# A two-block transformer on one core: `ada` sums of gMLP in later columns, residual tiles split where they are made, and VectorE's later work queued behind the first half's `diag`

## The chip, the cores and the metric

The kernel runs on one core of a Trainium2 chip. Of its engines four matter here. TensorE (PE in the profile; PEld is its weight load) multiplies. VectorE (DVE) and ScalarE (ACT) work on tiles and read what TensorE wrote into PSUM. SyncE's queue (SP) issues the loads from HBM. GpSimd (POOL) does a little elementwise work. The metric is the device time of one execution of the whole program in microseconds.

## The reference, cut to what matters

Two blocks run in one program, on 512 tokens of width 1024. The first has one layer. The second has two layers and a context of 256 tokens, and its two layers begin with different mixers.

```python
# first block, one layer
h = x + merged @ w_out                        # merged: two gated token mixers
hn = rmsnorm(h, norm2_g)
h = h + square(relu(hn @ w_ff1)) @ w_ff2
x = rmsnorm(h, final_g)
# second block, layers i = 0 (mla) and 1 (gmlp)
m = silu(c) @ ada_w[i] + ada_b[i]             # six vectors: shift, scale, gate, twice
x = x + gate_m * mixer(modulate(x, norm_mix_g[i], shift_m, scale_m))
x = x + gate_f * square(relu(modulate(x, norm_ffn_g[i], shift_f, scale_f) @ ffn_w1[i])) @ ffn_w2[i]
# gmlp
z = gelu(h @ w_in); u, v = z[:, :2048], z[:, 2048:]
v = layernorm(v)                              # over its 2048 features
out = (u * (ws @ v + bs)) @ w_out             # ws mixes tokens inside chunks of 128
```

`rmsnorm(x, g)` divides each token by the root of its mean square and multiplies by `g`; `modulate` is that norm, times `1 + scale`, plus `shift`.

## The kernel before, in words

**Tiles.** Activations lie transposed: the residual stream `h` is eight tiles of 128 features x 512 tokens. A product of float32 accuracy is made of three passes: each operand is split into a high part `hi` (rounded to a shorter format) and the rest `lo`, and `mm3` issues hi x hi, hi x lo and lo x hi for each of the eight slices of the inner dimension. A *column* is one output tile of 128 x 512: 24 products.

**Weights.** `wload` issues a load of 512 KB on SP's queue into one of three buffers `wr`, and splits it into `wh` (a copy on ScalarE) and `wl` (a subtraction on VectorE), with three buffers each. Activations are split the same way: `split_into` makes `hi` on ScalarE and `lo` on VectorE, with a gain multiplied in where one is given.

**Modulation vectors.** `ada` (L450) computes one slice of 128 entries of `m`: it loads 512 KB into a buffer of the same three `wr`, multiplies it by the row of silu(c) on VectorE and sums along the row (L461, output `adaj`). Layer 1 needs 48 such slices. The first 24 are made in other stages, by the table `ADA`; the remaining 24, n = 24 to 47, in the column loop of gMLP, one in an even column and two in an odd one, from column 0 on.

**Order.** The program is written as a trace of instructions, and a framework puts each engine's instructions in order by estimated times and priorities. Three devices change this. `soon` gives what is traced in its block a higher priority. Between `region` and `region_end` TensorE keeps the written order. `tc.issue_after(i)` makes what is traced in its block, on the engine of instruction `i`, come behind `i` in that engine's queue. Inside a region `later(n, f)` calls `f` after n further products counted in units of 256 moving columns, so that a product of 512 counts 2; `tick` counts them down. `first` multiplies the first columns of a stage one half of the tokens (256) at a time, for three weights, as the input tiles come.

**Norms.** `Sum` adds the squares of the tiles. `sums` sums them over the 128 features with products by ones, which gives a small tile of one value for each token. `rsqrt` computes the inverse root in it on VectorE, in eleven small instructions (a Newton iteration). `spread` brings the result back to all 128 partitions: VectorE multiplies the identity by it (`diag`), and TensorE multiplies ones by `diag` (L220).

**Layer ends.** `down` (L325) makes the last product of a layer. Its last tiles are made in two halves of 256 tokens, z = 0 and z = 1, so that the norm of the first half runs while TensorE makes the second half. `norm` collects the sums, and calls `done`, which computes the inverse root in the small tile; a later `spread` makes `diag` and its product, and then `modulate` makes the eight input tiles of the next stage for this half. The delays stand in `LATER`. This happens at four edges: behind the first feed-forward (`mlp_one`), behind the mla mixer's output, behind the feed-forward of layer 0 (`modulated_mlp(0)`), and behind gMLP.

**First feed-forward.** The loop over `w_out` (L806 to L816) makes the eight residual tiles, one column each, and adds their squares to `ss`. Then `mlp_one` splits all eight tiles, scaled by `g2`, and calls `mlp`, with `halves` false: its first columns are not written in an order of their own. The norm is applied to the output: every column of `ff1` passes through relu and is multiplied by the token's inverse root (`r2`). `scale` makes `r2` when the first column's output needs it. The sums, Newton iteration and spread of this norm are traced there.

**gMLP.** First `v` is made for all tokens, then normalised on VectorE (L1462), 16 tiles. Then the loop over the 16 columns of `u` runs. Each column has 24 products that need the input alone, and four products of 128 columns that need the normalised `v` of a fourth of the features.

Of the kernel before, what the change touches and what calls it, by code (L numbers as in the profile page):

```python
# [29 lines left out]
T = 512  # L30
# [55 lines left out]
class Kernel:  # L86
# [40 lines left out]
    def tt(self, out, a, b, op, eng=None):  # L127
        (eng or self.nc.vector).tensor_tensor(out=out, in0=a, in1=b, op=op)  # L128
# [64 lines left out]

    def region(self):
        self.due, self.open = [], self.tc.manual_schedule(engines={mybir.EngineType.PE})
        self.open.__enter__()

    def region_end(self):
        while self.due:
            self.due.pop(0)[1]()  # L200
        self.open.__exit__(None, None, None)
        self.due = self.open = None
# [89 lines left out]
    def spread(self, c, n=T, bank=None, i=0):  # L292

        k = n // 128
        d = self.S(n, name="diag")
        self.tt(d.rearrange("p (k c) -> p k c", c=128), self.ident[:, None, :].to_broadcast([128, k, 128]),
                c.rearrange("p (k two) -> p k two", two=2)[:, :, i:i + 1].to_broadcast([128, k, 128]), ALU.mult)
        ps = (bank or self.P)()
        self.mm(ps[:, :n], self.ones, d)
        return ps[:, :n]  # L300

# [23 lines left out]
    def down(self, srcs, rs, bank, residual, sums, done, whole=4, begun={}, wide=False):  # L325
# [12 lines left out]
        for z, c in enumerate(HALF):  # L338
            cols = self.O()
            for m in range(whole, 8)[::1 - 2 * z]:  # L340
# [13 lines left out]
                def norm(z=z, cols=cols, when=when):  # L354
                    with self.soon():
                        sums.collect(cols, z)
                        then = done(z, cols)

                        def spread():
                            with self.soon():  # L360
                                r = self.spread(then[0], TC, self.P, then[2])
                            then[1](r)
                        self.later(when[2 * z + 1], spread)
# [179 lines left out]
    def mlp(self, w1, w2, xs, residual, scale=None, extra=None, down=None, halves=True, fast=None):  # L543


        step = [0]

# [5 lines left out]
        def ff1(g, between=None):  # L553
            r = []
            for j in range(8):
                if g == 0 and halves:
                    if j == 0:
                        ps3 = [self.Q() for _ in range(3)]
                        self.first(ps3, [self.wsplit(self.wload(w1[i]), 8) for i in range(3)], xs)
                if g == 0 and halves and j < 3:  # L560
                    ps = ps3[j]
                else:
                    w = self.wload(w1[g * 8 + j])
                    ps = self.O() if j % 2 else self.P()
                    self.mm3(ps, self.wsplit(w, 8), xs)
                t = self.F(name="relu", tag="relu")
                if scale is None:
                    self.nc.vector.tensor_scalar(out=t, in0=ps, scalar1=0.0, scalar2=None, op0=ALU.max)
                else:
                    self.stt(t, ps, 0.0, scale(), ALU.max, ALU.mult)  # L570
# [88 lines left out]
    def mlp_one(self):  # L659
        nc, a, h = self.nc, self.a, self.x  # L660
        xs = [self.split(h[m], self.col("g2", m)) for m in range(8)]
        self.tap("h", h)
        ssq, r2 = self.ss, []

        def scale():
            if not r2:
                r = self.S(name="rstd")
                nc.scalar.copy(r, self.rstd(ssq.acc[0], 1024))
                r2.append(r)
            return r2[0]  # L670
# [24 lines left out]
        def done(z, cols):  # L695
            if z == 0:
# [11 lines left out]
        self.mlp(a["ff1"], a["ff2"], xs, residual, scale, extra,  # L708
                 (self.Sum(self, gains=g2), done), False)
        self.tap("h2", h)  # L710

    def mixer_one(self):
# [93 lines left out]
        self.x, self.ss = [], self.Sum(self)  # L806
        for m in range(8):
# [6 lines left out]
            self.tt(x, x, ps, ALU.add)  # L814
            self.ss.add(x)
            self.x.append(x)  # L816
# [607 lines left out]
    def gmlp(self, m):  # L1424
# [46 lines left out]
        for c in range(16):  # L1471
            for n in todo[:2 if c % 2 else 1]:
                self.ada(1, n, n + 1)
            del todo[:2 if c % 2 else 1]
# [113 lines left out]
```

## Time and profile before

| | |
|---|---|
| Median of 3 runs | 2113.36 us (2110.32 to 2115.81) |
| Profiled execution | 2112.48 us |
| Its span in the trace | 2110.8 us |
| Mean granted TensorE clock, share of full speed | 0.993 |
| TensorE busy | 2062.7 us, 98 % of the span |
| TensorE weight load | 85 % |
| VectorE | 71 % |
| ScalarE | 44 % |
| GpSimd | 10 % |
| Read from HBM | 232.70 MB, 112 GB/s over the span |
| Transfers of the load queue | 35.0 % of 16 DMA engines' span |

The span is the time from the first to the last instruction in the trace; the profiled execution's own time is a little more, by what lies around it. A busy share is a mean over the whole span. "Busy" of TensorE holds also the time in which it works at half its clock. The granted clock is given as a share of full speed, 2.4 GHz; 0.5 is the lower level, 1.2 GHz.

### The profile page before, as it was taken

How to read it: one execution, taken by the hardware profiler on the slowest of the kernel's cores; microseconds unless marked ns; L12 is line 12 of the kernel's file. 1: busy time of each engine (PE TensorE's matmuls, PEld its weight loads, DVE VectorE, ACT ScalarE, POOL GpSimd, SP SyncE). 2: the span in 40 equal slices, each digit the busy share in tenths (PEclk: the TensorE clock that was granted, in tenths of full speed). 3: DMA queues.
4: the chain of work that ended last, by engine and by line, in shares of the span. 5: the costliest groups of instructions: out<-in, count | busy, mean ns of one | idle time of the engine just before them, and what ended most of it. 6: DMA issues, size and time to landing. Idle time of an engine off the chain costs nothing.

```text
span 2110.8 us, 29897 instructions
## 1 busy us (share of the span) xinstructions
PE 2062.7 (98%) x11414; PEld 1788.3 (85%) x11414; DVE 1506.5 (71%) x2893; ACT 928.4 (44%) x1600; POOL 216.8 (10%) x234
## 2 busy tenths in 40 slices
PE   9999999999999999999989999999989999999999
PEld 7888888878888888889878898988877889899897
DVE  6868775689675557888869878776368547777673
ACT  5546663354242324666655434343323334444341
POOL 0313220000000001345411000000000001000000
PEclk9999999999999999999999999999999999999999
DMA  5212122556565532101032344443355431232232
GB/s 173 70 60 66 47 85 60 158 173 210 171 189 183 177 110 87 33 23 36 31 120 75 123 163 130 159 155 115 100 171 177 131 120 51 81 119 93 98 111 90
DMA packets 73921, 238.84 MB, mean 113 GB/s; under 512 B 8241, under 2 KB 12593, under 8 KB 73778
## 3 DMA queue, kind: packets, MB, share of 16 engines
q1 hardware_dynamic: 73778, 236.94, 35.0%
q8 instruction: 89, 1.46, 0.3%
q14 instruction: 54, 0.44, 0.1%
HBM read 232.70 MB, written 4.20 MB: 112 GB/s over the span
## 4 chain that ended last, share of the span: by engine, by line
PE 83%; DVE 9%; ACT 3%; DMA 3%; issue 2%; POOL 0%; SPq 0%; POOLq 0%; ACTq 0%; DVEq 0%
PE pq L189 32%; PE ps L189 27%; PE po L189 13%; PE pg L189 2%; DMA ada<-in_ada 2%; DVE wl L128 1%; PE sc L220 1%; PE pl L220 1%; ACT pr L134 1%; DVE mod L131 1%; PE z L189 1%; DVE adaj L461 1%; DVE lo L128 1%; PE o L189 1%; PE pq L220 1%
## 5 line engine op out<-in xcount | busy, mean ns | idle before, releaser
L139 ACT CAST wh<-wr 128x1024 fp32r<-128x1024 f32 (+3 forms) x362 | 324.8, 906 | 595.6 <-PE pq L189 258.3
L128 DVE TENSOR_TENSOR wl<-wr,wh 128x1024 fp32r<-128x1024 f32 (+3 forms) x362 | 378.0, 1051 | 86.7 <-ACT wh L139 83.5
L189 PE MATMUL pq<-hi,wl 128*128 128x512 f32 (+1 forms) x880 | 335.9, 383 | 0.0
L189 PE MATMUL pq<-lo,wh 128*128 128x512 f32 (+1 forms) x880 | 335.7, 383 | 0.0
L189 PE MATMUL pq<-hi,wh 128*128 128x512 f32 (+1 forms) x880 | 335.5, 383 | 0.0
L189 PE MATMUL ps<-hi,wh 128*128 128x512 f32 x536 | 212.4, 397 | 4.4 <-ACT hi L134 2.1
L189 PE MATMUL ps<-hi,wl 128*128 128x512 f32 x536 | 211.7, 395 | 0.5 <-DVE wl L128 0.5
L189 PE MATMUL ps<-lo,wh 128*128 128x512 f32 x536 | 210.9, 394 | 0.0
L461 DVE SCALAR_TENSOR_TENSOR adaj<-ada,silu 128x1024 bf16<-128x1024 f32 x112 | 136.9, 1222 | 100.3 <-DMA ada<-in_ada 100.0
L189 PEld LDWEIGHTS pq<-hi,wl 128*128 128x128 f32 x880 | 165.6, 188 | 32.2 <-DVE wl L128 0.6
L189 PEld LDWEIGHTS pq<-hi,wh 128*128 128x128 f32 x880 | 165.6, 188 | 31.3
L189 PEld LDWEIGHTS pq<-lo,wh 128*128 128x128 f32 x880 | 165.7, 188 | 30.7
L189 PE MATMUL ps<-hl,wh 128*128 128x256 f32 (+1 forms) x752 | 181.3, 332 | 1.8 <-DVE m L128 1.0
L128 POOL TENSOR_TENSOR hl<-mod,hl 128x256 fp32r<-128x256 f32 x36 | 30.6, 857 | 1169.0 <-ACT hl L387 951.0
L189 PEld LDWEIGHTS ps<-hl,wh 128*128 128x128 f32 x752 | 129.0, 191 | 16.8 <-DVE u L128 2.1
L131 DVE SCALAR_TENSOR_TENSOR x<-pq,m,x 128x512 f32<-128x512 f32 (+1 forms) x88 | 60.4, 687 | 96.9 <-PE pq L189 95.9
L189 PE MATMUL ps<-hl,wl 128*128 128x256 f32 (+1 forms) x376 | 124.1, 330 | 0.0
L189 PEld LDWEIGHTS ps<-hi,wh 128*128 128x128 f32 x536 | 100.8, 188 | 26.5 <-ACT hi L134 2.5
L189 PEld LDWEIGHTS ps<-hi,wl 128*128 128x128 f32 x536 | 101.0, 188 | 22.3 <-DVE wl L128 1.0
L189 PEld LDWEIGHTS ps<-lo,wh 128*128 128x128 f32 x536 | 101.1, 189 | 20.2 <-DVE lo L128 0.4
L189 PE MATMUL po<-hl,wh 128*128 128x256 f32 (+1 forms) x528 | 116.6, 315 | 0.0
L139 ACT CAST wh<-ws 128x512 fp32r<-128x512 f32 x96 | 56.8, 619 | 95.7 <-PE po L189 69.8
(409 smaller groups left out, 4542.9 us busy)
## 6 DMA issues: line engine op xcount, KB each, us to landing
wr<-in_f SPq DMA_DIRECT2D x128, 512.0 KB, 3.5
ada<-in_ada SPq DMA_DIRECT2D x96, 512.0 KB, 3.9
wr<-in_ff SPq DMA_DIRECT2D x64, 512.0 KB, 4.2
wr<-in_w_in SPq DMA_DIRECT2D x41, 512.0 KB, 3.5
wr<-in_gw_v SPq DMA_DIRECT2D x16, 512.0 KB, 3.5
wr<-in_gw_u SPq DMA_DIRECT2D x16, 512.0 KB, 4.0
wr<-in_gw_o SPq DMA_DIRECT2D x16, 512.0 KB, 3.5
wr<-in_w_out SPq DMA_DIRECT2D x8, 512.0 KB, 3.9
```

The lines of the kernel that those rows point to most:

```text
L128: (eng or self.nc.vector).tensor_tensor(out=out, in0=a, in1=b, op=op)
L131: (eng or self.nc.vector).scalar_tensor_tensor(out=out, in0=a, scalar=s, in1=b, op0=op0, op1=op1)
L134: self.nc.scalar.activation(out=out, in_=x, func=func, scale=scale, bias=bias, **k)
L139: nc.scalar.copy(hi, x)
L189: self.nc.tensor.matmul(out, l, r, start=start and i == j == 0, stop=stop and i == n - 1 and j == 2, **k)
L220: self.nc.tensor.matmul(out, l, r, start=start, stop=stop)
L461: nc.vector.scalar_tensor_tensor(out=d, in0=w, scalar=1.0, in1=s, op0=ALU.mult, op1=ALU.mult, accum_out=m[:, n:n + 1])
```

## The change

There are three parts.

1. `down` and `mlp_one` make `diag` directly behind the inverse root, no longer at the time of the spread. For the first half (z = 0) `hold` opens a block of `issue_after` behind this `diag`, which is closed by `region_end`: all of VectorE's work that is traced until then stands behind `diag` in VectorE's queue. To this end `tt` returns its instruction, and `spread` is cut into `diag` on VectorE and `spread_diag` on TensorE.
2. The residual tiles are split inside the `w_out` loop, each as soon as it is made and ahead of its square. `mlp` takes `begin = (count, start)` in place of `halves`. For the first feed-forward, count is 2 and `start` writes TensorE's order: for each of the eight tiles three products into one column and three into a second. The sums come 26 units behind the start, which is 13 products, and the spread 44 units behind those, which is 22. `r2` is written by ScalarE from the spread.
3. In gMLP no `ada` sum stands in columns 0 to 3; from column 4 on each column has two, until the 24 are done at column 15.

```diff
     def tt(self, out, a, b, op, eng=None):
-        (eng or self.nc.vector).tensor_tensor(out=out, in0=a, in1=b, op=op)
+        return (eng or self.nc.vector).tensor_tensor(out=out, in0=a, in1=b, op=op)
     def stt(self, out, a, s, b, op0, op1, eng=None):
         (eng or self.nc.vector).scalar_tensor_tensor(out=out, in0=a, scalar=s, in1=b, op0=op0, op1=op1)
...
+    def hold(self, d):
+        self.held.enter_context(self.tc.issue_after(d[1].ins))
     def region(self):
+        self.held = ExitStack()
         self.due, self.open = [], self.tc.manual_schedule(engines={mybir.EngineType.PE})
         self.open.__enter__()
     def region_end(self):
         while self.due:
             self.due.pop(0)[1]()
+        self.held.close()
         self.open.__exit__(None, None, None)
         self.due = self.open = None
...
             self.stt(b, b, -0.5, a, ALU.mult, ALU.mult)
             self.stt(out, b, 1.5, out, ALU.add, ALU.mult)
-    def spread(self, c, n=T, bank=None, i=0):
+    def diag(self, c, n=T, i=0):
         k = n // 128
         d = self.S(n, name="diag")
-        self.tt(d.rearrange("p (k c) -> p k c", c=128), self.ident[:, None, :].to_broadcast([128, k, 128]),
-                c.rearrange("p (k two) -> p k two", two=2)[:, :, i:i + 1].to_broadcast([128, k, 128]), ALU.mult)
-        ps = (bank or self.P)()
+        return d, self.tt(d.rearrange("p (k c) -> p k c", c=128), self.ident[:, None, :].to_broadcast([128, k, 128]),
+                          c.rearrange("p (k two) -> p k two", two=2)[:, :, i:i + 1].to_broadcast([128, k, 128]), ALU.mult)
+    def spread_diag(self, d, bank=None):
+        ps, n = (bank or self.P)(), d.shape[-1]
         self.mm(ps[:, :n], self.ones, d)
         return ps[:, :n]
+    def spread(self, c, n=T, bank=None, i=0):
+        return self.spread_diag(self.diag(c, n, i)[0], bank)
     def rstd(self, acc, d, n=T, bank=None):
...
                     with self.soon():
                         sums.collect(cols, z)
                         then = done(z, cols)
+                        d = self.diag(then[0], TC, then[2])
+                        if z == 0:
+                            self.hold(d)
                         def spread():
                             with self.soon():
-                                r = self.spread(then[0], TC, self.P, then[2])
+                                r = self.spread_diag(d[0], self.P)
                             then[1](r)
                         self.later(when[2 * z + 1], spread)
                 self.later(when[2 * z], norm)
...
         self.tt(u[0][:, a1], y[:, a0], v, add)
         return u
-    def mlp(self, w1, w2, xs, residual, scale=None, extra=None, down=None, halves=True, fast=None):
+    def mlp(self, w1, w2, xs, residual, scale=None, extra=None, down=None, begin=None, fast=None):
         step = [0]
+        count, start = begin or (3, lambda ps, ws: self.first(ps, ws, xs))
         def tick():
             if extra:
...
         def ff1(g, between=None):
             r = []
             for j in range(8):
-                if g == 0 and halves:
-                    if j == 0:
-                        ps3 = [self.Q() for _ in range(3)]
-                        self.first(ps3, [self.wsplit(self.wload(w1[i]), 8) for i in range(3)], xs)
-                if g == 0 and halves and j < 3:
-                    ps = ps3[j]
+                if g == j == 0:
+                    begun = [self.Q() for _ in range(count)]
+                    start(begun, [self.wsplit(self.wload(w1[i]), 8) for i in range(count)])
+                if g == 0 and j < count:
+                    ps = begun[j]
                 else:
                     w = self.wload(w1[g * 8 + j])
                     ps = self.O() if j % 2 else self.P()
...
                 if scale is None:
                     self.nc.vector.tensor_scalar(out=t, in0=ps, scalar1=0.0, scalar2=None, op0=ALU.max)
                 else:
-                    self.stt(t, ps, 0.0, scale(), ALU.max, ALU.mult)
+                    self.stt(t, ps, 0.0, scale, ALU.max, ALU.mult)
                 self.act(t, t, AF.Square)
                 r.append(self.split(t, tag="f"))
                 if between:
...
     def mlp_one(self):
         nc, a, h = self.nc, self.a, self.x
-        xs = [self.split(h[m], self.col("g2", m)) for m in range(8)]
+        xs, r2 = self.xs, self.S(name="rstd")
         self.tap("h", h)
-        ssq, r2 = self.ss, []
-        def scale():
-            if not r2:
-                r = self.S(name="rstd")
-                nc.scalar.copy(r, self.rstd(ssq.acc[0], 1024))
-                r2.append(r)
-            return r2[0]
+        def norm():
+            c = self.small()
+            with self.soon():
+                self.rsqrt(c, self.sums(self.ss.acc[0], T, self.O), 1024)
+                d = self.diag(c)
+                self.hold(d)
+            def spread():
+                with self.soon():
+                    nc.scalar.copy(r2, self.spread_diag(d[0], self.O))
+            self.later(44, spread)
+        def start(ps, ws):
+            self.region()
+            self.later(26, norm)
+            for k in range(8):
+                for p, w in zip(ps, ws):
+                    self.mm3(p, w[k:k + 1], xs[k:k + 1], k == 0, k == 7)
+            self.region_end()
         self.ada_begin()
         g2 = self.kp.tile([128, 16], F32, tag="g2", name="g2").rearrange("p (k two) -> p k two", two=2)
         nc.vector.memset(g2[:, :, 0:1], 1.0)
...
             v.tensor_copy(out=self.c1[:, 4 * z:4 * z + 4], in_=e)
             return e, lambda r: self.modulate(self.xs, h, r, gs, m0[:, 0:8], HALF[z]), 1
         self.h = h
-        self.mlp(a["ff1"], a["ff2"], xs, residual, scale, extra,
-                 (self.Sum(self, gains=g2), done), False)
+        self.mlp(a["ff1"], a["ff2"], xs, residual, r2, extra, (self.Sum(self, gains=g2), done), begin=(2, start))
         self.tap("h2", h)
     def mixer_one(self):
...
                 do["GM"[b] + str(m)] = lambda b=b, m=m: branch(b, m)
         for what in ORDER.split():
             do[what]()
-        self.x, self.ss = [], self.Sum(self)
+        self.x, self.xs, self.ss = [], [], self.Sum(self)
         for m in range(8):
             hl = self.wload(a["w_out"][m])
             with tc.issue_after(self.last_load.ins):
...
             ps = self.P()
             self.mm3(ps, self.wsplit(hl, 8), merged)
             self.tt(x, x, ps, ALU.add)
+            self.x.append(x)
+            self.xs.append(self.split(x, self.col("g2", m)))
             self.ss.add(x)
-            self.x.append(x)
     def sb_pair(self, p, do, feat, qz, vz, out):
...
         um = []
         todo = list(range(len(ADA[1]), 48))
         for c in range(16):
-            for n in todo[:2 if c % 2 else 1]:
+            for n in todo[:2] if c >= 4 else ():
                 self.ada(1, n, n + 1)
-            del todo[:2 if c % 2 else 1]
+                todo.remove(n)
             w = self.wload(a["gw_u"][c])
             ps = self.P()
             self.mm3(ps, self.wsplit(w, 8), xs)
```

## Rows read from the trace of the kernel before

**Rows 1.** Engines' busy time on the page: busy us (share of the span) xinstructions.

```profile
PE 2062.7 (98%) x11414; PEld 1788.3 (85%) x11414; DVE 1506.5 (71%) x2893; ACT 928.4 (44%) x1600; POOL 216.8 (10%) x234
```

**Rows 2.** What TensorE waited for: us in total, times, longest us.

```profile
PE pq L220 <- DVE v L1462: 8.4, 4, 4.5
...
PE ps L189 <- ACT hi L134: 2.1, 1, 2.1
...
PE ps L220 <- DVE diag L128: 1.8, 2, 1.6
```

**Rows 3.** Windows around the first feed-forward: length, PE, PEld, DVE, ACT, POOL, clock, DMA.

```profile
393.70:432.40 38.70, 38.70 (x169) 31.27 (x167) 16.90 (x20) 11.33 (x15) 0.00 (x0) 1.00 0.45 142
...
434.60:441.60 7.00, 7.00 (x21) 5.71 (x22) 6.97 (x19) 6.41 (x14) 0.00 (x0) 0.51 0.76 262
```

**Rows 4.** Timeline, end of `w_out` and start of the first feed-forward, three engines.

```profile
433.42 1.23 DVE L128 TENSOR_TENSOR wl<-wr,wh 128x1024 fp32r<-128x1024 f32 x1 [0.21 <-ACT wh L139]
...
433.83 3.16 ACT L134 ACTIVATE hi<-h,cols 128x512 fp32r<-128x512 f32 x5
...
434.59 0.68 PE L189 MATMUL ps<-hi,wh 128*128 128x512 f32 x1 [2.10 <-ACT hi L134]
...
437.23 0.17 DVE L279 TENSOR_SCALAR ra<-ps 128x8 f32<-128x8 f32 x1
```

**Rows 5.** Chain that ended last, first feed-forward: start us, us, what.

```profile
435.70 1.50 PE ps L220 x8
...
450.34 0.86 PE ps L220 x2
```

**Rows 6.** Groups of VectorE's instructions from 434.6 to 451.

```profile
L131 DVE SCALAR_TENSOR_TENSOR lo<-h,cols,hi 128x512 fp32r<-128x512 f32 x8 | 5.8, 744 | 0.0
...
L128 DVE TENSOR_TENSOR sq<-sq 128x256 f32<-128x256 f32 x7 | 2.9, 418 | 0.1
...
L128 DVE TENSOR_TENSOR silu<-silu,sg 128x512 f32<-128x512 f32 x4 | 2.6, 679 | 0.0
```

**Rows 7.** Windows, the `u` columns of gMLP.

```profile
1557.60:1672.50 114.90, 106.45 (x515) 89.44 (x514) 89.61 (x204) 34.62 (x49) 0.00 (x0) 0.96 0.55 173
...
1582.10:1591.90 9.80, 6.93 (x24) 5.98 (x25) 9.29 (x21) 0.38 (x1) 0.00 (x0) 0.50 0.55 165
...
1627.80:1640.60 12.80, 12.80 (x66) 10.83 (x65) 10.46 (x20) 4.26 (x8) 0.00 (x0) 1.00 0.67 188
```

**Rows 8.** Groups of VectorE's instructions from 1558.5 to 1588.4.

```profile
L461 DVE SCALAR_TENSOR_TENSOR adaj<-ada,silu 128x1024 bf16<-128x1024 f32 x7 | 8.6, 1222 | 4.8 <-DMA ada<-in_ada 4.8
...
L1462 DVE TENSOR_SCALAR v<-v,mv,rv 128x512 f32<-128x512 f32 x16 | 7.6, 539 | 0.0
```

**Rows 9.** Timeline, first layer edge, VectorE and TensorE.

```profile
791.08 0.16 DVE L700 TENSOR_SCALAR c<-po 128x4 f32<-128x4 f32 x1 [0.86 <-PE po L220]
...
796.06 0.42 DVE L128 TENSOR_TENSOR diag<-ident,c 128x256 f32<-128x256 f32 x1
...
796.53 0.70 PE L220 MATMUL ps<-diag,ones 128*128 128x256 f32 x2 [1.56 <-DVE diag L128]
...
804.28 0.50 PE L189 MATMUL pl<-hl,wh 128*128 128x256 f32 x2 [0.82 <-DVE h L128]
...
806.68 0.16 DVE L700 TENSOR_SCALAR c<-po 128x4 f32<-128x4 f32 x1 [0.80 <-PE po L220]
...
809.33 1.02 DVE L128 TENSOR_TENSOR diag<-ident,c 128x256 f32<-128x256 f32 x2
```

**Rows 10.** Windows, the first layer edge.

```profile
791.00:804.30 13.30, 10.92 (x88) 10.46 (x87) 11.75 (x37) 7.02 (x17) 2.91 (x4) 1.00 0.17 60
```

**Rows 11.** Chain that ended last, two undisturbed columns of gMLP.

```profile
1602.26 5.49 PE ps L189 x24
...
1608.64 5.49 PE ps L189 x24
```

**Rows 12.** DMA issues from 1595 to 1660: KB each, median us to landing.

```profile
wr<-in_gw_u SPq DMA_DIRECT2D x8, 512.0 KB, 4.2
```

## The prediction, made before the changed kernel was run

> **What bounds the kernel now.** The page comes first: TensorE is busy for 98 per cent of the span [rows 1]. So the span shrinks only where TensorE stands still or runs at half speed. The list of what TensorE waited for, longest first, says where that is [rows 2]: 8.4 us in four waits for the normalised `v` of gMLP, the longest 4.5, and one wait of 2.1 us for the split `hi`. Next the tables of windows show what the granted clock did after these: it stood at 0.51 from 434.6 to 441.6 [rows 3] and at 0.50 from 1582.1 to 1591.9 [rows 7], which is the lower of its two levels, 1.2 instead of 2.4 GHz. The timelines and the groups of VectorE's instructions in these stretches then say what was late [rows 4, 6, 8, 9].
>
> **The change part by part.** It has three parts, at three kinds of places.
>
> *First feed-forward, residual tiles split as made.* Now TensorE stands 2.10 us before its first product there, and what ends it is ScalarE's first `hi` [rows 4]. The `hi` instructions start only behind the last square, although seven of the eight residual tiles are long done. The 7.0 us at 0.51 that follow hold some 3.6 us of work at full speed, so 3.4 us are lost. Idle and clock together are 2.1 + 3.4 = 5.5 us, the ceiling of this part. After the change each tile's `hi` (0.63 us on ScalarE, a fifth of the row of five) and `lo` (0.74 us on VectorE [rows 6]) are issued inside the `w_out` loop. That stage is 38.7 us long, and VectorE is busy for 16.9 of it, ScalarE for 11.3 [rows 3]; eight times 0.74 and 0.63 us fit and cost nothing. Without that cover they would cost up to 5.9 us. The same move takes seven of the eight `lo`, 5.2 us, from VectorE behind 434.6, where it is busy 6.97 of 7.00 us [rows 3]. That matters: TensorE can come several us earlier there only because VectorE has that much less to do.
>
> What is late next is the norm, since TensorE now follows a written order. The sums come after 13 products, the spread after 22 more. At 5.49 us for 24 products [rows 11], one is 0.23 us. TensorE, starting at 432.5 instead of 434.59, reaches the sums at 435.5. The weights' `wl` holds VectorE to 434.65 [rows 4], then come `lo` (0.74) and the square's sum (0.68 as for a `silu` product of the same shape [rows 6]): 436.1, a wait of 0.6 us. The eight products of the sums took 1.50 us at the low clock [rows 5]; I take 1.0 us, so they end at 437.1, and the spread is due 22 products later, at 442.1. The norm's chain on VectorE is 2.65 us from its first instruction (806.68) to `diag` (809.33) when nothing comes between [rows 9]; with 0.7 us for a `diag` of 512 columns it is ready near 440.6. But now the chain that starts at 437.23 [rows 4] feeds a spread only at 450.34 [rows 5]: other work stands between its links. The tiles' `lo` are gone from there; the squares of the context (2.9 us), the `silu` products (2.6) [rows 6] and one `ada` sum (1.2 [rows 8]) remain, 6.7 us. `soon` puts the chain ahead of them but cannot stop one that has begun. I take 2.3 us of them, so 0.8 us of wait, between none and 5.2 us (all of them). The part gives 5.5 - 0.6 - 0.8 = 4.1 us. The order that `hold` writes here covers only products, so it costs nothing.
>
> A row bears on these two short waits. In the window from 791.0 to 804.3, with two waits of 1.56 and 0.82 us [rows 9], the clock stayed at 1.00 [rows 10]. By that, short waits cost themselves only, and 4.1 us stands. The Trainium skill, "TensorE: Matmul & The Clock Gate", section "A second HAM failure mode: psum-queue depth-cycling", says that frequent small idle stretches are enough to throttle again. By this the part would lose another fall of the clock, 3.4 us, and the sum below would be 12.7 us; the trace so far speaks against it. It is one of the rivals.
>
> *gMLP, `ada` sums later.* The 16 columns of `u` take 114.9 us [rows 7]. An undisturbed column is 1608.64 - 1602.26 = 6.38 us [rows 11], 16 of them 102.1 us. The 12.8 us between are the ceiling: 8.4 us of waits for `v`, some 3.5 us of half clock (6.93 us of busy TensorE at 0.50), the rest small. The groups of rows 8 are those of VectorE from ScalarE's last `v`, 1558.5, to the last normalised one, 1588.4: seven `ada` sums stand there with 8.6 us, and VectorE is idle for 4.8 us more until their loads land, with later work behind them. After the change no sum belongs to columns 0 to 3. Without these 13.4 us the last `v` is normalised at 1575.0. TensorE has three columns of products that need no `v`: 1557.6 + 3 x 5.49 = 1574.1. The loads for columns 4 and 5 can still start as soon as a buffer is free, so I let three sums (3.7 us) come early, half of it hidden by the fourth column's products: some 1.8 us of wait stay. The part gives 11.0 us, between 6 (half the sums still come early) and 12.8.
>
> The 24 sums then go two to a column, from the fourth column on. Two columns now hold three sums and 10.46 us of VectorE in 12.80 [rows 7]; a fourth of 1.2 us makes 11.7, which fits. On SP's queue a column has three loads through three `wr` buffers. A buffer is held for the landing, 4.2 us [rows 12], and then for its use: 1.2 us for a sum [rows 8], 2.3 us for a weight (a cast of about 1.1, as the 1.2 us of `wl` [rows 4]). With 0.3 us of issue between, a column holds buffers for 2 x 5.7 + 6.8 = 18.2 us, 6.1 us for each of the three, under its 6.38. I cost it at nothing; above that it costs what is over, less the lead of the weights.
>
> *Layer ends, VectorE's later work behind the first half's `diag`.* At the first edge the chain takes 4.98 us to `diag` [rows 9], 2.65 when free: 2.3 us of other work, a `wl` above all, stand inside. TensorE waits 1.56 us for `diag` there. With the hold that goes, but the other work comes behind, and VectorE is busy 11.75 of the 13.3 us [rows 10]; TensorE then waits at 804.28 for the last addition, 0.82 us, and that wait grows. Only VectorE's idle time in the stretch can be won: I take 0.6 us. Of the 1.8 us of waits for `diag` [rows 2] only 0.2 lie at the other edges; I take 0.4 us there, with some of VectorE's idle time. The part gives 1.0 us. Its ends: 2.4 us if both waits of the first edge go whole, -1.2 us if the displaced `wl` is missed once by TensorE.
>
> **Sum.** 4.1 + 11.0 + 1.0 = 16.1 us. The profiled execution took 2112.48 us around its span of 2110.8; 2112.48 - 16.1 = 2096.4. The median of the runs shown, 2113.36, is 0.9 us above the profiled one: 2097.3 us.
>
> **Rivals.**
> 1. *The spread comes too late* (0.13). All 6.7 us of other work stand in the chain, TensorE waits 5.2 us in its written order and the clock falls once more. For it: the spread came only at 450.34 before. Against: `soon`, and the `lo` are gone. The first part is then 5.5 - 0.6 - 5.2 - 3.4 = -3.7 us, the whole 8.3: 2105.1 us.
> 2. *The `ada` sums don't go later* (0.15). Their loads are issued when a buffer is free, not when the column comes; half of the seven stay ahead of `v`. The second part is 6 us, the sum 11.1: 2102.3 us.
> 3. *The clock falls at short waits* (0.08). The waits for the sums and the spread lie close together in the first feed-forward and bring the low clock once more, as the idle 2.10 us did: 3.4 us less, 12.7 us, 2100.7 us. What rows 10 show speaks against it.
> 4. *Slower: loads bound the columns* (0.03). With three loads a column, a landing of L us makes a column (3L + 5.6) / 3 us. Three `wh` buffers let the weights run some two columns, 10 us, ahead, and the other gains are 16.1 us. To end 6.3 us above the old median, 12 columns must lose 32 us, 2.7 each: L = 7.2 us. The row shows 4.2.
> 5. *Other stages are reordered* (0.06). The order on each engine comes from estimated times, so attention may change too: 6 us either way about the forecast.
>
> **How the numbers follow.** The forecast has 0.55, with 2093 to 2101 as its own range. The ceilings together, 5.5 + 12.8 + 2.4 = 20.7 us, give 2092.7; rivals 1 to 3 reach to 2105.1. The range 2091 to 2107 leaves out rival 4, the worse part of 1 and 5, and a little below. A measurement here tells about 0.3 per cent, 6.3 us, so faster means below 2107.0: all of the forecast, 2 and 3, half of 1, most of 5, 0.86. Within 0.3 per cent: the rest of 1 and 5 and mixtures of 1 and 2, 0.10. Slower: 0.04.
>
> **What would show it.** Right: no wait for `hi` near 432, the clock at 1.00 through the first feed-forward's start, a spread wait under 2 us; in gMLP the waits for `v` under 2.5 us, 16 columns in about 104 us, VectorE near 91 per cent from the fourth column; at the first edge no wait for `diag`, a longer one behind it. Wrong: a new wait of several us for `diag` in the first feed-forward, `ada` sums still standing between the last `v` and its normalisation, columns longer than 6.4 us late in gMLP, or a changed attention stage.

## The result and the profile after

The changed kernel takes 2126.32 us (median of 5 runs, 2122.42 to 2128.95), the kernel before 2114.64 us (5 runs, 2110.32 to 2115.81). The ratio is 1.0057, with a 95 % interval of 1.0046 to 1.0067: 10 to 14 us slower, where 16.1 us faster was forecast. The profiled execution has a span of 2124.6 us, 13.8 more than before.

The engines' busy time on the page of the changed kernel, against [rows 1]:

```profile
PE 2067.2 (97%) x11414; PEld 1794.0 (84%) x11414; DVE 1506.2 (71%) x2893; ACT 927.7 (44%) x1600; POOL 215.3 (10%) x234
```

The work is the same; TensorE has 4.5 us more of busy time and the rest of the 13.8 us is standing. What it waited for in the changed kernel, longest first (total, times, longest), against [rows 2]:

```profile
PE po L226 <- DVE sq L128: 11.0, 6, 3.5
PE po L226 <- DVE diag L128: 7.7, 1, 7.7
PE pq L226 <- DVE v L1490: 4.8, 1, 4.8
```

The wait for `hi` is gone and three of the four waits for `v`. New are 7.7 us for `diag` and long waits for the squares (`sq`), which took 2.4 us in all before.

**First feed-forward.** Windows of the changed kernel around its norm, with the columns of [rows 3]:

```profile
438.00:446.50 8.50, 8.50 (x42) 6.88 (x40) 8.50 (x26) 2.09 (x7) 0.00 (x0) 1.00 0.58 170
446.50:454.30 7.80, 0.07 (x1) 0.00 (x0) 6.82 (x21) 0.93 (x1) 0.00 (x0) 0.79 0.54 166
454.30:462.00 7.70, 7.69 (x25) 5.58 (x26) 4.87 (x9) 3.38 (x5) 0.00 (x0) 0.77 0.42 117
```

VectorE is busy for 6.82 of the 7.80 us in which TensorE stands, from 446.5 to 454.3. The clock falls inside this wait (mean 0.79) and is not yet back behind it (0.77). VectorE's timeline in the stretch, from the chain's first link to `diag`, and TensorE's product of the spread:

```profile
441.16 0.16 DVE L285 TENSOR_SCALAR ra<-po 128x8 f32<-128x8 f32 x1
441.30 1.22 DVE L476 SCALAR_TENSOR_TENSOR adaj<-ada,silu 128x1024 bf16<-128x1024 f32 x1
...
450.88 1.23 DVE L476 SCALAR_TENSOR_TENSOR adaj<-ada,silu 128x1024 bf16<-128x1024 f32 x1 [0.83 <-DMA ada<-in_ada]
...
453.56 0.69 DVE L128 TENSOR_TENSOR diag<-ident,c 128x512 f32<-128x512 f32 x1
...
454.31 2.08 PE L226 MATMUL po<-diag,ones 128*128 128x512 f32 x2 [7.74 <-DVE diag L128]
```

The chain takes 12.4 us from its first link to `diag` (441.16 to 453.56). The groups of VectorE's instructions from 441.1 to 454.3 say what stands between its links:

```profile
L476 DVE SCALAR_TENSOR_TENSOR adaj<-ada,silu 128x1024 bf16<-128x1024 f32 x6 | 7.3, 1224 | 0.8 <-DMA ada<-in_ada 0.8
L128 DVE TENSOR_TENSOR sq<-sq 128x256 f32<-128x256 f32 x6 | 2.5, 423 | 0.0
L128 DVE TENSOR_TENSOR wl<-wr,wh 128x1024 fp32r<-128x1024 f32 x1 | 1.2, 1223 | 0.0
```

**Layer ends.** VectorE's and TensorE's timelines at the four edges, in order: the next stage's weight splits (`wl`) in one row, then the sums of the second half's squares with the wait ahead of them:

```profile
799.20 0.42 DVE L128 TENSOR_TENSOR diag<-ident,c 128x256 f32<-128x256 f32 x1
...
799.86 3.49 DVE L128 TENSOR_TENSOR wl<-wr,wh 128x1024 fp32r<-128x1024 f32 x3
...
812.50 1.66 PE L226 MATMUL po<-sel,sq 128*128 128x2 f32 x8 [3.53 <-DVE sq L128]
...
1114.85 3.48 DVE L128 TENSOR_TENSOR wl<-wr,wh 128x1024 fp32r<-128x1024 f32 x3
...
1126.81 1.01 PE L226 MATMUL po<-ones,sq 128*128 128x2 f32 x4 [2.77 <-DVE sq L128]
...
1470.26 3.48 DVE L128 TENSOR_TENSOR wl<-wr,wh 128x1024 fp32r<-128x1024 f32 x3
...
1482.14 1.01 PE L226 MATMUL po<-ones,sq 128*128 128x2 f32 x4 [1.69 <-DVE sq L128]
...
1766.65 3.49 DVE L128 TENSOR_TENSOR wl<-wr,wh 128x1024 fp32r<-128x1024 f32 x3
...
1777.28 0.61 PE L226 MATMUL po<-ones,sq 128*128 128x2 f32 x4 [1.78 <-DVE sq L128]
```

At the first edge the chain is as short as forecast: `diag` stands at 799.20, 2.66 us behind the chain's first link at 796.54 (4.98 in [rows 9]). But three splits come right behind it. Windows of that edge, up to `diag`, then the second half's products, the wait and what follows:

```profile
791.00:799.20 8.20, 8.20 (x72) 8.20 (x70) 4.70 (x21) 1.88 (x3) 0.00 (x0) 1.00 0.00 0
799.20:808.90 9.70, 9.59 (x76) 9.08 (x74) 9.70 (x21) 4.88 (x12) 1.67 (x3) 1.00 0.56 191
808.90:812.50 3.60, 0.07 (x1) 0.00 (x0) 3.60 (x9) 1.57 (x5) 1.44 (x2) 1.00 0.00 0
812.50:819.60 7.10, 7.10 (x34) 7.10 (x35) 3.57 (x17) 0.00 (x0) 0.00 (x0) 0.52 0.00 0
```

VectorE is idle for 3.5 us ahead of `diag`, full for the 13.3 us behind it, and TensorE's 3.6 us of wait are followed by 7.1 us at 0.52.

**gMLP.** Groups of VectorE's instructions from 1574.5 to 1597.9, up to the last normalised `v`, against [rows 8], and the windows of TensorE's wait and of what follows:

```profile
L476 DVE SCALAR_TENSOR_TENSOR adaj<-ada,silu 128x1024 bf16<-128x1024 f32 x6 | 7.3, 1225 | 2.3 <-DMA ada<-in_ada 2.3
```

```profile
1594.00:1597.90 3.90, 0.00 (x0) 0.00 (x0) 3.90 (x9) 0.00 (x0) 0.00 (x0) 0.99 0.41 145
1597.90:1602.00 4.10, 4.05 (x15) 3.63 (x16) 3.28 (x8) 0.00 (x0) 0.00 (x0) 0.59 0.75 261
```

Six sums, which belong to columns 4 and later, still stand ahead of the last `v`.

**Ledger.** Landmarks are products that both traces have. The spread of the context's norm, in the first feed-forward, comes at 578.07 us in place of 574.43: 3.6 us lost. From the first half's `diag` product to the second half's, the four edges take 19.39, 18.90, 17.32 and 13.96 us in place of 13.27, 13.98, 12.37 and 11.09: 18.9 us lost, less the 1.8 us of waits for `diag` in [rows 2]. From the start of gMLP's second `ws` product to the end of the last one with `v` it takes 185.6 us (1498.00 to 1683.57) in place of 190.8 (1481.75 to 1672.51): 5.2 us won. Together that is 15.5 us lost; the other 1.7 us, to the 13.8 of the spans, are won elsewhere and were not followed. The largest difference outside the ledger lies between the first edge and the second: 295.28 us from the one's last `diag` product to the other's first, in place of 299.54. And the share of the edges is that of one execution: in the traces of ff_ada_behind and v_ada_behind (below), which have the same hold there, the four edges together take 62.0 and 65.1 us, here 69.6, in the kernel before 50.7.

### The profile page after: what moved, and what is told of

Read it like the earlier page. It is cut to its first block, busy times and chain, and to the rows that moved or that the text cites. A ratio compares the mean times of both kernels' runs of the same rounds, so it can differ in the third digit from the quotient of the medians.

```text
span 2124.6 us, 29884 instructions
## 1 busy us (share of the span) xinstructions
PE 2067.2 (97%) x11414; PEld 1794.0 (84%) x11414; DVE 1506.2 (71%) x2893; ACT 927.7 (44%) x1600; POOL 215.3 (10%) x234
## 4 chain that ended last, share of the span: by engine, by line
PE 71%; DVE 13%; DMA 8%; issue 4%; ACT 3%; POOL 0%; SPq 0%; POOLq 0%; ACTq 0%; DVEq 0%
PE pq L189 31%; PE ps L189 20%; PE po L189 10%; DMA ada<-in_ada 7%; DVE wl L128 3%; PE pg L189 2%; DVE adaj L476 2%; PE sc L226 1%; PE pl L226 1%; ACT pr L134 1%; DVE lo L128 1%; DVE mod L131 1%; PE po L226 1%; ACT wh L139 1%; PE z L189 1%
## 5 line engine op out<-in xcount | busy, mean ns | idle before, releaser
L189 PE MATMUL pq<-hi,wl 128*128 128x512 f32 (+1 forms) x896 | 343.4, 384 | 0.5 <-DVE wl L128 0.5
L189 PE MATMUL pq<-lo,wh 128*128 128x512 f32 (+1 forms) x896 | 342.3, 383 | 0.0
L189 PE MATMUL pq<-hi,wh 128*128 128x512 f32 (+1 forms) x896 | 342.1, 383 | 0.0
```

Source lines behind the costliest of these rows:

```text
L189: self.nc.tensor.matmul(out, l, r, start=start and i == j == 0, stop=stop and i == n - 1 and j == 2, **k)
```

## The experiments

Each was timed in five rounds beside the kernel before. "Faster" and "slower" are against the kernel before, unless it is said otherwise. The intervals of the ratios are 95 %. Differences from the changed kernel are differences of medians from separate rounds; the kernel before had 2112.5 to 2114.6 us in these, so they are sure to about 2 us.

**Each part alone, and the whole without the hold.**

```diff
 # only_hold: before, with diag and hold in down()
+                        d = self.diag(then[0], TC, then[2])
+                        if z == 0:
+                            self.hold(d)
 # only_split: before, with the split in the w_out loop and begin=(2, start); norm() without hold
 # only_ada: before, with the new loop of ada sums in gmlp()
 # no_hold_edges: after, in down()
                         d = self.diag(then[0], TC, then[2])
-                        if z == 0:
-                            self.hold(d)
```

> The kernel before with the hold at the four layer edges as the one change. Theory A (displaced splits): the hold puts three weight splits of VectorE, 3.5 us, which the kernel before has done up to 20 us earlier, behind the first half's diag and so ahead of the second half's squares. TensorE then waits 1.7 to 3.5 us for the last square at each edge, and the granted clock falls to 0.5 behind it. Price by the four steps of the lag between the two traces (4.3, 4.4, 5.2 and 3.0 us): 12 to 17 us slower than before. Rival B (the other parts shifted the order, the hold is innocent): within 4 us of before, no wait above 1 us for the squares at the edges.

Measured: 2124.42 us, ratio 1.0062 (1.0049 to 1.0074), some 13 us slower. Its waits for the squares are those of the changed kernel:

```profile
PE po L226 <- DVE sq L128: 10.8, 6, 3.1
```

> The changed kernel without the hold at the four layer edges; diag is still made at once, the other parts stay, also the hold in the first feed-forward. Theory A (the hold costs the edges): 12 to 17 us faster than the changed kernel, 2109 to 2114 us, no wait above 1 us for the squares at the edges and a clock of 1.00 there. Rival B (diag made early, or the other parts, cost the edges): within 4 us of the changed kernel, 2122 us or more.

Measured: 2113.01 us, ratio 1.0004 (0.9995 to 1.0013), 13 us faster than the changed kernel. The waits for the squares are short again:

```profile
PE po L226 <- DVE sq L128: 3.2, 5, 0.8
```

Half to half, the four edges of this kernel take 13.25, 13.98, 12.37 and 11.10 us, those of before within 0.02. So the hold makes the edges slow; `diag` made early does not.

> The kernel before with the residual tiles split inside the loop, and the first two columns and the norm's products in written order, as the one change; nothing is held. Theory A: ada sums of VectorE, whose loads land early, stand between the links of the norm's chain, TensorE waits 5 to 12 us for diag and the clock falls: 2 to 8 us slower than before. Rival B (the splits and the order are sound, only the hold disturbs): 3 to 5 us faster, with a wait for diag below 2 us.

Measured: 2118.36 us, ratio 1.0030 (1.0018 to 1.0042), 6 us slower, with a wait of 7.85 us for `diag` at 454.61 behind six sums in the chain. Theory A holds; the change's own hold made no difference to that wait (7.74 us in the changed kernel), since the sums are traced after the region has ended and lifted it.

> The kernel before with the later ada sums of gMLP as the one change. Theory A: the loads go out as soon as a buffer is free, whatever the column, so about six sums still stand ahead of the last normalised v; the gain is what the lag of the two traces shows there, 6.4 us, so 5 to 8 us faster than before. Rival B (what was forecast): 11 us faster, at most three sums ahead of v.

Measured: 2109.84 us, ratio 0.9988 (0.9979 to 0.9997), 2.5 us faster. The same stretch as in the ledger takes 187.7 us (1482.33 to 1670.05), 3.0 less than before. Six sums stand ahead of `v`, as theory A has it, and a wait of 4.7 us for it is left; of what is won there, two waits for ScalarE's `gu` in the last columns, 0.64 us at 1648.62 and 1.70 at 1656.97, take 2.3 back, which theory A didn't have.

**Only the displaced work taken out.** The next stage's first three weights (wherever `wload` is called between `down` and `region_end`) are traced outside the held block; the second half's own work stays in it.

```diff
     def hold(self, d):
-        self.held.enter_context(self.tc.issue_after(d[1].ins))
+        self.behind = d[1].ins
+        self.held.enter_context(self.tc.issue_after(self.behind))
+    def exempt(self, srcs):
+        self.held.close()
+        ws = [self.wsplit(self.wload(x), 8) for x in srcs]
+        if self.due is not None:
+            self.held.enter_context(self.tc.issue_after(self.behind))
+        return ws
...
-                    start(begun, [self.wsplit(self.wload(w1[i]), 8) for i in range(count)])
+                    start(begun, self.exempt([w1[i] for i in range(count)]))
 # in mla() and gmlp() likewise
```

> The changed kernel, with the next stage's first weights' splits on VectorE exempt from the hold at the four layer edges; everything else stays behind the first half's diag. Theory A (the three displaced splits, 3.5 us, make the second half's squares late): waits for the squares at 1 us or less, clock at 1.00, 8 to 14 us faster than the changed kernel, 2112 to 2118 us. Rival B (VectorE's sum in the stretch decides, or the modulation that now comes ahead of the squares does): at least two edges keep a wait above 1.5 us for the squares, and 4 us or less are won.

Measured: 2115.43 us, ratio 1.0009 (1.0000 to 1.0017), 11 us faster than the changed kernel. VectorE's splits at the first edge, and TensorE's sums behind them with the window that follows:

```profile
779.15 1.23 DVE L128 TENSOR_TENSOR wl<-wr,wh 128x1024 fp32r<-128x1024 f32 x1 [0.22 <-ACT wh L139]
784.59 1.23 DVE L128 TENSOR_TENSOR wl<-wr,wh 128x1024 fp32r<-128x1024 f32 x1 [0.21 <-ACT wh L139]
799.97 1.23 DVE L128 TENSOR_TENSOR wl<-wr,wh 128x1024 fp32r<-128x1024 f32 x1 [0.43 <-ACT wh L139]
801.98 0.42 DVE L128 TENSOR_TENSOR diag<-ident,c 128x256 f32<-128x256 f32 x1
...
812.25 1.05 PE L235 MATMUL po<-sel,sq 128*128 128x2 f32 x8 [1.55 <-DVE sq L128]
```

```profile
812.25:816.40 4.15, 4.15 (x34) 4.06 (x34) 2.95 (x17) 0.00 (x0) 0.00 (x0) 1.00 0.00 0
```

Two of the splits shown are 17 us and more ahead of `diag`, in idle time of VectorE; the third stands inside the chain again, as in the kernel before. The wait for the squares is longer than expected, 1.55 us (1.24 at the second edge), but the clock stays at 1.00. So the displaced splits are the cause; the hold over the rest is worth nothing that shows.

**The sums kept out of the chain and out of the way of v.**

```diff
 # ff_ada_behind: after, in mlp_one(); norm_one is diag's instruction
                 if ADA[0][n] == i:
-                    self.ada(0, n, n + 1)
+                    with self.tc.issue_after(self.norm_one):
+                        self.ada(0, n, n + 1)
 # the context's steps likewise
 # v_ada_behind: after, in gmlp(); vn is the last normalisation
             for n in todo[:2] if c >= 4 else ():
-                self.ada(1, n, n + 1)
+                with self.tc.issue_after(vn.ins):
+                    self.ada(1, n, n + 1)
```

> The changed kernel, with the ada sums and the context's work of the first feed-forward queued behind the norm's diag as well (they are traced after the region ends, so the change's own hold doesn't reach them). Theory A (these sums stand between the links of the chain): the wait of 7.7 us for diag falls below 1 us, the clock stays at 1.00, and the stage gives about 8 us: 2116 to 2120 us. Rival B (the sums hold the raw weight buffers while they stand behind, and the next columns' weights come late): the wait moves to the weights and 0 to 4 us are won: 2122 us or more.

Measured: 2119.34 us, ratio 1.0028 (1.0017 to 1.0040), 7 us faster than the changed kernel. VectorE's chain, and TensorE's spread, which no longer waits:

```profile
441.08 0.17 DVE L285 TENSOR_SCALAR ra<-po 128x8 f32<-128x8 f32 x1 [2.73 <-PE po L226]
...
443.30 0.69 DVE L128 TENSOR_TENSOR diag<-ident,c 128x512 f32<-128x512 f32 x1
443.91 1.22 DVE L476 SCALAR_TENSOR_TENSOR adaj<-ada,silu 128x1024 bf16<-128x1024 f32 x1
...
446.50 1.02 PE L226 MATMUL po<-diag,ones 128*128 128x512 f32 x2
```

> The changed kernel, with gMLP's ada sums queued behind the last normalised v on VectorE. Theory A (six sums and the idle time for their loads, 9.6 us, keep v late): the wait of 4.8 us for v goes, with some 2 us of low clock behind it: 5 to 7 us faster than the changed kernel, 2119 to 2121 us. Rival B (their loads still go out early and keep two of the three raw buffers until VectorE comes to the sums, so the columns' weights are late): 2 us or less, or slower, with waits for weights in columns 3 to 5.

Measured: 2115.75 us, ratio 1.0015 (1.0006 to 1.0024), 10.6 us faster than the changed kernel. In the trace gMLP's stretch is 178.2 us (1491.50 to 1669.68), 7.4 less than in the changed kernel; the rest isn't from gMLP (see the end).

> The kernel before with the later ada sums of gMLP, queued behind the last normalised v, as the one change. Theory A (11 us were to be had if the sums really went later): 9 to 13 us faster than before, no wait above 1 us for v, the clock at 1.00 through the columns. Rival B (12 columns with two sums each run into the loads or VectorE's limit): 6 us faster or less.

Measured: 2100.27 us, ratio 0.9938 (0.9925 to 0.9950), 13 us faster. The 16 columns of `u` in this kernel, against the first of [rows 7]. They begin at 1558.36 and end at 1660.61 us, so that the window is 1.15 us longer than they are:

```profile
1557.60:1661.00 103.40, 103.40 (x520) 87.50 (x519) 92.88 (x211) 34.47 (x50) 0.00 (x0) 1.00 0.68 207
```

The columns take 102.3 us, about the 102.1 of 16 undisturbed ones. No wait and no low clock is left; VectorE, with 90 per cent, and the loads carry two sums to a column.

**The first feed-forward's part by itself, and the parts together.**

> The kernel before with the tiles split in the loop and the written order, and with the ada sums and the context's work of that stage behind diag; gMLP and the layer edges as before. Theory A (the forecast of 4.1 us for this part was right in its terms; only the sums in the chain were missed): 2 to 4 us faster than before, less what the displaced sums cost at the weights' splits (waits for wl of some 2 us). Rival B (the displaced sums take it all back): within 1 us of before.

Measured: 2112.42 us, ratio 0.9998 (0.9989 to 1.0007): no difference. Edit: only_split with the block of ff_ada_behind.

```diff
 # best1: no_hold_edges + ff_ada_behind + v_ada_behind
 # best2: weights_exempt + ff_ada_behind + v_ada_behind
 # best3: best1, but each sum of the first feed-forward behind its own column's relu
-                    with self.tc.issue_after(self.norm_one):
+                    with self.tc.issue_after(self.at):
```

> The changed kernel without the hold at the four layer edges, with the ada sums of the first feed-forward behind its diag and those of gMLP behind the last v. Theory A (the three causes add up): 2113 less 8 and 6, 2097 to 2101 us. Rival B (waits move on to weights or to the loads that the sums' buffers keep out): 2106 us or more.

Measured: 2101.84 us, ratio 0.9949 (0.9937 to 0.9962), 11 us faster and 0.8 above the range of theory A. A window of this kernel in the first feed-forward, behind the spread:

```profile
460.00:480.00 20.00, 18.91 (x82) 14.76 (x81) 19.79 (x38) 9.89 (x14) 0.00 (x0) 1.00 0.61 196
```

VectorE is full: the sums that were put behind `diag` are done here, and TensorE stands 1.09 us for splits of weights, in two waits of 0.28 and 0.81 us.

> The hold at the edges with the next stage's first weights exempt, and the ada sums behind diag and behind the last v. It differs from the version without a hold at the edges (2102 us) by the exempt hold alone. Theory A (VectorE is full behind the first half's diag, so what the chain gains the squares lose): within 3 us of 2102. Rival B (a free chain is worth the forecast 1 us or more once the weights are out of the way): 2099 us or less.

Measured: 2100.84 us, ratio 0.9941 (0.9928 to 0.9953). Within the interval of best1: an exempt hold brings nothing that can be measured.

> No hold at the edges, gMLP's ada sums behind the last v, and each ada sum of the first feed-forward behind its own column's relu in place of the norm's diag, so that they cannot gather right behind diag, where VectorE is full (19.8 of 20.0 us) and TensorE waits about 2 us for weight splits. Theory A (crowding behind diag costs these waits): 2098 to 2100 us. Rival B (the raw buffers that waiting sums hold make the weights late, wherever the sums stand): 2101 to 2105 us.

Measured: 2129.32 us, ratio 1.0073 (1.0060 to 1.0087), 27 us slower than best1. What TensorE waited for in it:

```profile
PE ps L189 <- ACT wh L139: 12.6, 4, 5.7
PE po L189 <- ACT wh L139: 5.7, 3, 3.2
```

Weights come late, by more than rival B said. From 450 to 540 us 25 loads of weights and sums were issued, 35 in best1: a sum that waits for its column keeps a raw buffer, which the next weight's load needs. That reading rests on these counts; it was not tested further.

```diff
 # split_late and best4: split_behind and best2 with a later table
-ADA = ((2, 2, 3, 4, 5, 6, 8, 8, 9, 9, ...
+ADA = ((6, 7, 8, 9, 10, 11, 12, 13, 14, 15, ...
```

> The kernel before with the tiles split in the loop, the written order and the ada sums of that stage behind diag, and the table of those sums starting at column 6 in place of 2, about one to a column. Theory A (sums crowded behind diag cost the waits for weight splits): no wait above 0.5 us for a split in that stage, 4 to 6 us ahead of before at its end; with the first edge undisturbed 2108 to 2110 us, with its low clock 2111 to 2113. Rival B (VectorE's work there is too much wherever it stands): again about 1 us ahead at the stage's end and 2112 us or more.

Measured: 2117.01 us, ratio 1.0021 (1.0013 to 1.0030), slower. The waits for splits between 450 and 540 us are gone, as theory A has it, but a longer one stands behind them, where the context's weights are loaded:

```profile
571.75 0.80 PE L189 MATMUL po<-hi,wl 128*128 128x512 f32 x1 [4.10 <-DVE wl L128]
```

> The version with the exempt hold and the sums behind diag and behind v (2101 us), with the same later table. Theory A: the stage ends 2 to 4 us earlier than in that version, 2096.5 to 2099 us. Rival B: 2100 us or more.

Measured: 2103.53 us, ratio 0.9954 (0.9940 to 0.9968), no faster than best2, for the same reason (a longest wait of 3.6 us for `wl`). Theory A's times fell in both runs. Rival B's times held (2112 us or more, 2100 or more), but not its reading: from 561 to 576 us of split_late VectorE is busy for only 8.35 of 15.0 us. The load of the context's weight goes out there at 565.90 us, behind that of a sum at 563.98, and its cast begins at 570.30: the crowd moved on to the loads. This is read from one trace and was not tested.

## Why the prediction was wrong

1. **Layer ends: this step failed, and decides the sign.** Forecast 1.0 us won, ends 2.4 and -1.2; measured alone 13 us lost. The step said that VectorE's idle time in the stretch can be won and that a displaced `wl` costs 1.2 us if it is missed once. The chain did shrink to 2.66 us. But the hold catches all that is traced until `region_end`, and that has three splits, 3.5 us, of which the kernel before does two ahead of the norm, at 772.4 and 777.9 us, in VectorE's idle time. I priced the one that stands inside the chain in [rows 9], counted none of the others, and left out that the squares stand behind them. And I priced a lost wait at its own length. In the profiled execution the clock stood near 0.5 for some 7 us behind the first three waits, as from 812.5 to 819.6 above, which costs 3.4 us of work; behind the fourth, 1.78 us, the mean was 0.69 for 5.5 us. (In other executions with the same hold it was less; see the last section.) That the three other edges have the same queue was not worked out at all.

2. **First feed-forward: rival 1 came true, with a longer wait.** Forecast 4.1 us won; the part alone lost 6. The idle time for `hi` and its low clock went, as forecast. The failed step is the list of work between the chain's links, 6.7 us with one `ada` sum in it. There were six sums, 7.3 us, and the wait was 7.7, not 0.8. The list was taken from the trace of before, where VectorE was busy with the tiles' `lo`, and even there two sums stand in the chain, at 446.31 and 447.56 us; the 5.2 us that were taken away were filled again by sums of later columns, as soon as their loads had landed (for one VectorE stood 0.83 us). That `hold` covers only products here and costs nothing was right, and for that very reason it did not protect the chain. A second slip changed nothing: the last `w_out` column runs behind the first 13 products, so that the sums came at 440.0 and not 435.5, and the chain was due at 446.5. With the sums behind `diag` the chain was ready at 444.0, with room to spare.

3. **That part's ceiling.** Even so it gave nothing (split_behind): VectorE is full behind `diag` and what was won at the start is given back at the weights' splits, and in that run at the first edge: the spread comes 2.6 us earlier than before and the edge's first `diag` product 1.6 us, but the edge itself takes 3.9 us longer, with a wait of 1.76 us for the squares and a clock of 0.52 behind it. I had treated VectorE's work there as free once it was off the chain.

4. **gMLP: rival 2 came true.** Forecast 11.0 us, rival 2 said 6; 5.2 in the trace of the changed kernel, 2.5 as a part alone. The step that failed is that "no sum belongs to columns 0 to 3", with three let in early: a place in the written loop holds back neither a load nor a sum, and six came. The rest of the working held: with the sums tied behind the last `v` the columns took 102.3 us (forecast about 104) at a clock of 1.00, and the kernel gained 13 us, where the ceiling was 12.8. The loads of 18.2 us for three buffers did fit.

5. **The rivals.** No rival had the hold as a loss; the slower case, 0.04, rested on loads that bound gMLP's columns, which didn't happen. Rivals 1 and 2 came together, 0.13 and 0.15, and would have given about 2110 us; the hold's 13 us, in place of 1 us won, make most of the rest of the way to 2126. Rival 3 didn't show: the two short waits in the window 460 to 480 us of best1, 1.09 us together, left the clock at 1.00. The Trainium skill, "TensorE: Matmul & The Clock Gate", section "A second HAM failure mode: psum-queue depth-cycling", says that frequent small idle stretches throttle; two waits in 20 us hardly test that.

What stays open is why the first edge keeps its clock in one version and loses it in another with nearly the same order. Waits of 1.55 us in weights_exempt and of 1.56 in [rows 9] left it at 1.00; behind 1.76 us in split_behind it fell to a mean of 0.52 over 7.1 us, and behind only 1.53 us in best2 to 0.69 over 5.6 us. So the length of the wait alone doesn't decide. It was not tried to bring that wait to a set length.

## What to carry to other kernels

Before a chain is given priority by a barrier in an engine's queue, list everything that is traced behind the barrier until it is lifted, also the next stage's weights, and sum it against the other engine's work in that stretch: what was done early in idle time becomes late all at once. Where a framework orders by estimated times, a later place in the program's text delays little; tie the late work to the instruction that it must not overtake (2109.84 us became 2100.27 by one line), and to none later than that: best3 suggests, by its counts of loads, that work that waits keeps its buffers. The best versions here, ada_behind (2100.27 us) and best2 (2100.84 us), gain almost all from that one tie.

## What the runs showed of the hardware

In the changed kernel one wait of TensorE at each of the four edges, 1.69 to 3.53 us long, was followed by 5.5 to 7.2 us at a mean granted clock of 0.51 to 0.69, so that with the work lost there it cost two to three times its length. But the same wait doesn't cost the same in each execution. ff_ada_behind has the four waits too (3.55, 2.76, 1.68 and 1.78 us), and behind the last two its clock stayed at 1.00. The fourth edge in the changed kernel and in ff_ada_behind, 34 products behind a wait of 1.78 us in each:

```profile
1777.30:1782.80 5.50, 5.50 (x34) 5.50 (x35) 2.56 (x13) 0.07 (x1) 0.77 (x1) 0.69 0.01 3
1766.74:1770.77 4.03, 4.03 (x34) 4.03 (x34) 2.56 (x13) 0.08 (x1) 0.78 (x1) 1.00 0.02 4
```

The clock also fell where TensorE didn't wait. In the kernel before, 20 products of two columns each, which the profile shows as busy time, came ahead of such a fall:

```profile
834.56 0.95 PE L220 MATMUL ps<-ones,sq 128*128 128x2 f32 x8
835.37 1.48 PE L220 MATMUL ps<-sel,pe 128*128 128x2 f32 x12
...
836.50:841.00 4.50, 4.50 (x16) 3.57 (x16) 4.43 (x9) 0.00 (x0) 2.50 (x2) 0.62 0.18 60
```

Four or eight products of this kind also come directly behind each wait for the squares, and none behind the wait for `diag` of [rows 9], which left the clock at 1.00. How the fall at an edge is shared between the wait and these products was not tested.

And single executions differ more than expected: the changed kernel and v_ada_behind have the same order of instructions up to gMLP, yet at its second `ws` product one trace stands at 1498.00 and the other at 1491.50 us. 4.5 of these 6.5 us come from the first three edges, whose waits for the squares are the same and are followed by means of 0.70, 0.69 and 0.71 over 5.5 to 5.8 us in v_ada_behind, in place of some 7 us near 0.5. A difference of a few microseconds between two traces, outside the stretch that an edit touches, says nothing by itself.
